# Second norm of a transformer block: the last expert's rows stay on chip and reach their tokens through TensorE, the other experts' sums are added in PSUM

## The chip, the core and the metric

One core of a Trainium2 chip runs the whole block. Measured is the device time of one execution in microseconds (us); the kernel before has a median of 1298.9 us over three runs (1298.69 to 1301.45). Engines are called PE or TensorE (matrix products), ACT or ScalarE, DVE or VectorE, POOL or GpSimd and SP (which only issues DMAs). Each runs its own list of instructions strictly in order and waits on semaphores for the others.

## The reference

One layer: a mixer of sparse attention and gated linear attention, a layer norm, a mixture of 32 experts (two for each token), a second layer norm. What the change touches is the end:

```python
h = layer_norm(DEEPNORM_ALPHA * h + mix, ln1_g[l], ln1_b[l])
...
y = lax.ragged_dot(jax.nn.silu(hg) * hu, w_e_out, sizes)
out = jnp.zeros_like(xt).at[tok_s].add(y * gate_s[:, None].astype(y.dtype))
...
h = layer_norm(DEEPNORM_ALPHA * h + ffn, ln2_g[l], ln2_b[l])
```

There are 1024 tokens of 1024 float32 values. An expert multiplies the rows of its tokens with a 1024x1024 and a 512x1024 matrix; its results, weighted with a gate, are added to the tokens' rows, and the norm is taken over each row.

## The kernel before

The 1024 tokens are 8 tiles of 128. `out_phase` makes the first norm and the router and writes two tables to device memory: `d_h` (the rows, which experts gather) and `d_y` (the rows times alpha, onto which the experts' results are added).

`expert_stream` runs the 32 experts one behind the other, in an order written by hand for PE, ACT and DVE. Each weight piece (1 MB, float32) is loaded by SP, split into a high part on ACT (line 180) and a low part on DVE (line 181), and used in three PE products (line 1351) per 512 columns. `second(e, ...)` makes the second product of expert e, while the first product of expert e+1 is already done; `results` (lines 1398 to 1405) takes the two halves of the 128 result rows out of PSUM, with the gate, one half on ACT (line 1402) and one on DVE (line 1403), into a tile `y`, and POOL issues an indirect DMA that adds them to `d_y` (line 1404). These scatters go one after the other: POOL waits until the one before has landed, since both may add to the same row.

Behind the last expert stands `more_blocks`, a loop (line 1499) that runs only if an expert has more than 128 tokens; here it runs zero times. All engines meet at its entry, and what is behind it starts when the scatter of expert 31 has landed.

`last_norm` then reads `d_y` in 8 loads of 512 KB (line 1558, all issued by SP). While they come, PE spreads the gain and the shift of the norm over 128 partitions, with 8 plain float32 products of 8 partitions and 256 columns (line 1330, issued in `experts`), and ACT copies them from PSUM (line 1565) for POOL. For each tile t the string `LAST[t]` says who does what. Its first letter is the statistics: A on ACT (line 1572 sums the row, line 1575 sums the squares), D on DVE (lines 1581 to 1584). The power -0.5 of the variance is always on POOL (`rstd`, lines 498 and 499). The other two letters are the halves of 512 columns: D stands for two DVE instructions (lines 1602 and 1603), P, G and S for one ACT instruction (line 1605) and two further ones for gain and shift on POOL (line 1610) or DVE (line 1608). The result goes out from the tile by SP (lines 1612 and 1614). The statistics of tile t+1 are begun (`next(gens[t + 1])`) before those of tile t are finished. The order in `last_norm` is that of the program text, but a list scheduler may move instructions within an engine.

## Time and profile before

| | us |
|---|---|
| median of 3 runs | 1298.9 |
| the profiled execution | 1299.05 |
| its span (first to last instruction) | 1297.3 |
| TensorE busy in the span | 1207.5 |
| last product of the last expert issued | 1255.51 |
| scatter of the last expert landed | 1265.72 |
| first load of the last norm issued | 1266.67 |
| end of the span | 1297.3 |

The page gives, for one execution, the busy time of each engine, the span in 40 slices, the chain of waits that ended last, and groups of instructions by source line. Times in the trace count from the start of the span. "PEclk" is the TensorE clock that was granted as a share of 2.4 GHz: 1.00 is 2.4 GHz, 0.50 is 1.2 GHz. A row of the timeline has start, duration, engine, line, operation, output and inputs, shape, and how many instructions were merged into it; matrix products overlap, so that the distance of two starts is what one costs in a stream, not its duration.

### The profile page before, as it was taken

How to read it: one execution, taken by the hardware profiler on the slowest of the kernel's cores; microseconds unless marked ns; L12 is line 12 of the kernel's file. 1: busy time of each engine (PE TensorE's matmuls, PEld its weight loads, DVE VectorE, ACT ScalarE, POOL GpSimd, SP SyncE). 2: the span in 40 equal slices, each digit the busy share in tenths (PEclk: the TensorE clock that was granted, in tenths of full speed). 3: DMA queues.
4: the chain of work that ended last, by engine and by line, in shares of the span. 5: the costliest groups of instructions: out<-in, count | busy, mean ns of one | idle time of the engine just before them, and what ended most of it. 6: DMA issues, size and time to landing. Idle time of an engine off the chain costs nothing.

```text
span 1297.3 us, 19390 instructions
## 1 busy us (share of the span) xinstructions
PE 1207.5 (93%) x6926; PEld 1006.5 (78%) x6926; DVE 1029.1 (79%) x1657; ACT 792.0 (61%) x1111; POOL 388.1 (30%) x350
## 2 busy tenths in 40 slices
PE   6999999999996999999959999999999999999962
PEld 5979989877795888888847888888888888888851
DVE  4567898999993566467768998899988999889855
ACT  4378366665425666122247777777777777777745
POOL 2532642355751453011121312122212222122115
PEclk9999999999997999899969999999999999999985
DMA  7653544324468651784377999999999999999926
GB/s 256 162 180 98 195 156 132 98 70 135 130 172 233 194 163 59 264 295 163 138 274 277 369 365 367 386 368 365 375 358 374 354 357 352 353 357 345 330 68 259
DMA packets 134356, 322.61 MB, mean 249 GB/s; under 512 B 20953, under 2 KB 51570, under 8 KB 134258
## 3 DMA queue, kind: packets, MB, share of 16 engines
q1 hardware_dynamic: 109826, 280.92, 60.8%
q0 software_dynamic: 14848, 25.22, 7.8%
q10 hardware_dynamic: 9584, 15.21, 3.5%
q8 instruction: 55, 0.90, 0.3%
q14 instruction: 43, 0.35, 0.1%
HBM read 283.78 MB, written 54.26 MB: 261 GB/s over the span
## 4 chain that ended last, share of the span: by engine, by line
PE 75%; DVE 9%; DMA 8%; ACT 4%; issue 2%; POOL 1%; SPq 0%; POOLq 0%; ACTq 0%; DVEq 0%
PE acc L1351 25%; PE ot L1351 12%; PE acc L1055 7%; PE acc L236 7%; PE acc L222 6%; DVE eq L722 3%; PE pt L1418 3%; PE s L835 3%; DMA d_y<-y,tok 2%; PE ot L873 2%; PE pt L859 2%; DMA big<-we 2%; PE g L236 1%; PE ot L1070 1%; DMA d_mix<-ym 1%
## 5 line engine op out<-in xcount | busy, mean ns | idle before, releaser
L181 DVE TENSOR_TENSOR elo<-big,ehi 128x2048 fp32r<-128x2048 f32 (+1 forms) x132 | 268.1, 2061 | 22.6 <-ACT ehi L180 21.9
L180 ACT CAST ehi<-big 128x2048 fp32r<-128x2048 f32 (+1 forms) x132 | 223.1, 1727 | 1.9 <-DMA big<-wf 1.2
L1351 PE MATMUL acc<-ehi,xh 128*128 128x512 f32 x512 | 207.4, 405 | 2.0 <-ACT sg L1467 2.0
L1351 PE MATMUL acc<-elo,xh 128*128 128x512 f32 x512 | 204.2, 399 | 0.0
L1351 PE MATMUL acc<-ehi,xl 128*128 128x512 f32 x512 | 204.0, 398 | 0.0
L1425 POOL DMA_INDIRECT xg<-d_h,tok x32 | 36.8, 1150 | 362.4 <-PE pt L1418 361.9
L222 PE MATMUL acc<-big,whi 128*128 128x512 f32 (+1 forms) x384 | 119.4, 390 | 10.5 <-ACT big L180 10.5
L236 PE MATMUL acc<-whi,big 128*128 128x256 f32 x672 | 125.9, 286 | 0.0
L1404 POOL DMA_INDIRECT d_y<-y,tok x32 | 93.0, 2906 | 109.7 <-ACT ehi L180 50.3
L1351 PEld LDWEIGHTS acc<-ehi,xh 128*128 128x128 f32 x512 | 97.3, 190 | 24.7 <-ACT sg L1467 2.4
L1351 PEld LDWEIGHTS acc<-ehi,xl 128*128 128x128 f32 x512 | 97.2, 190 | 23.8 <-DVE xl L181 0.3
L1351 PEld LDWEIGHTS acc<-elo,xh 128*128 128x128 f32 x512 | 97.6, 191 | 22.1
L236 PEld LDWEIGHTS acc<-whi,big 128*128 128x128 f32 x672 | 106.1, 192 | 1.9 <-issue 1.2
L722 DVE TENSOR_SCALAR_CACHE_REDUCE eq<-sc,cand 128x384 bf16<-128x384 f32 (+1 forms) x124 | 100.5, 811 | 6.9 <-POOL sc L734 4.6
L1351 PE MATMUL ot<-ehi,ah 128*128 128x512 f32 x256 | 104.1, 407 | 0.4 <-ACT ah L180 0.4
L181 DVE TENSOR_TENSOR elo<-slot,ehi 128x2048 fp32r<-128x2048 f32 (+1 forms) x46 | 95.6, 2101 | 9.2 <-ACT ehi L180 9.0
L1351 PE MATMUL ot<-ehi,al 128*128 128x512 f32 x256 | 101.6, 397 | 0.4 <-DVE al L181 0.4
L1351 PE MATMUL ot<-elo,ah 128*128 128x512 f32 x256 | 101.5, 396 | 0.0
L236 PE MATMUL acc<-wlo,big 128*128 128x256 f32 x336 | 95.9, 286 | 0.0
L752 ACT ACTIVATE sn<-sc,cand 128x896 bf16<-128x896 f32 (+1 forms) x62 | 67.9, 1095 | 45.8 <-DVE cand L748 34.9
L222 PEld LDWEIGHTS acc<-big,whi 128*128 128x128 f32 x384 | 71.7, 191 | 25.4 <-ACT big L180 10.5
L1055 PE MATMUL acc<-wohi,m 128*128 128x512 f32 x256 | 87.8, 413 | 0.0
(295 smaller groups left out, 2598.0 us busy)
## 6 DMA issues: line engine op xcount, KB each, us to landing
big<-we SPq DMA_DIRECT2D x79, 1024.0 KB, 17.5
big<-wf SPq DMA_DIRECT2D x40, 1024.0 KB, 21.3
slot<-we SPq DMA_DIRECT2D x26, 1024.0 KB, 19.5
sc<-we SPq DMA_DIRECT2D x20, 1024.0 KB, 15.8
slot<-wf SPq DMA_DIRECT2D x16, 1024.0 KB, 14.0
wraw<-wi SPq DMA_DIRECT2D x52, 256.0 KB, 3.2
sc<-wf SPq DMA_DIRECT2D x8, 1024.0 KB, 12.9
raw<-xT SPq DMA_DIRECT2D x8, 512.0 KB, 6.9
```

Of the source, the lines that this page charges most:

```text
L180: nc.scalar.copy(hi, src)
L181: (lo_eng or nc.vector).tensor_tensor(lo, src, hi.bitcast(F32), op=OP.subtract)
L222: nc.tensor.matmul(ps[:m, :n], l[:, j, c0:c0 + m], r[:, j % 2, t0:t0 + n], start=(j == 0 and a == 0), stop=(j == 7 and a == 2))
L236: nc.tensor.matmul(ps[:, i, :], l[:, j % 2, s], r[:, j, :], start=(j == 0 and a == 0), stop=(j == 7 and a == 2))
L722: nc.vector.tensor_scalar(gtt[:, :WS[i]], x, v, 0.0, op0=op, op1=OP.add, accum_out=cnt[:, i:i + 1])
L752: nc.scalar.activation(jnk[:, :WS[i]], y[i], AF.Sign, bias=c, accum_out=cnt[:, i:i + 1])
L835: nc.tensor.matmul(ps[:, 512 * c:512 * c + mm], lq, kk[hd][:, a, c0:c0 + mm], start=a == 0, stop=a == 1)
L1055: nc.tensor.matmul(ps, l[:, j, :], w[:, j, s], start=(j == 0 and a == 0), stop=(j == 7 and a == 2))
L1351: nc.tensor.matmul(o, x[:, jj, :], w[:, j, s], start=(jj == 0 and a == 0), stop=(jj == n - 1 and a == 2))
L1404: nc.gpsimd.indirect_dma_start(out=self.d_y, out_offset=bass.IndirectOffsetOnAxis(ap=tok.bitcast(U32), axis=0), in_=y, in_offset=None, bou ...
L1418: self.last_mm = nc.tensor.transpose(pt[:, 128 * i:128 * i + 128], src[:, 128 * (b + i):128 * (b + i) + 128], self.c["ident"])
L1425: self.last_gather = nc.gpsimd.indirect_dma_start(out=xg, out_offset=None, in_=self.d_h, in_offset=bass.IndirectOffsetOnAxis(ap=tok.bitcas ...
```

## The change

Expert 31 no longer scatters. `places` (called in the middle of its second product) makes, on DVE, for each of the 8 token tiles a 128x128 matrix `sel` of zeros and ones that says which of the expert's rows belongs to which token, and has SP load gain and shift, broadcast to 128 partitions, into a weight buffer that is free by then. `keep_rows` takes the expert's result rows out of PSUM as a high part (ACT) and a low part (DVE) into an SBUF tile `y31`. Expert 30 takes both halves of its rows out on ACT.

`last_norm` has its own PSUM: one pair of banks `sh` for the shift (4 products instead of 8; the gain is now read from SBUF) and three pairs `r2` for tiles of 128x1024. `last_expert()` puts `sel` times `y31` into the next pair (four products of 512 columns, in the one-pass float32r format of the experts' products); `others(t)` adds the tile of `d_y` to it (two plain float32 products of 512 columns with the identity matrix). The statistics and the first step of the normalisation read the sum from PSUM. `last_expert` is called for the first three tiles ahead of everything, and for tile t+3 after the work on tile t. The loads of `d_y` are issued by SP and ACT in turn. In `LAST` the last tile is "ASS" instead of "AGS". The slots of `raw_of` in the loop that runs zero times are shifted by two. The diff, without `raw_of` and the moved banks:

```diff
-LAST = ("ADP", "DDD", "APP", "DDD", "ADD", "ADD", "ADD", "AGS")
+LAST = ("ADP", "DDD", "APP", "DDD", "ADD", "ADD", "ADD", "ASS")
...
-            self.results(ys, cols(e))
+            if e < NE - 1:
+                self.results(ys, cols(e), e == NE - 2)
+            else:
+                self.keep_rows(ys, cols(e)[1])
...
-        second(NE - 1, last)
-
-    def results(self, ys, cols):
+        second(NE - 1, last, self.places)
+
+    def places(self):
+        nc = self.nc
+        self.y31 = self.big(F32R)
+        self.sel = self.big(F32R)[:, 0].rearrange("p (t c) -> p t c", c=128)
+        for t in range(NT):
+            nc.vector.tensor_scalar(self.sel[:, t, :], self.c["iota"], self.lists[:, NE - 1, 0:1], float(PAD - 128 * t),
+                                    op0=OP.subtract, op1=OP.is_equal)
+        self.gain, self.shift = self.slots[8][:, 0], self.slots[8][:, 1]
+        for i, o in enumerate((self.gain, self.shift)):
+            nc.sync.dma_start(o, self.I["l2"][i:i + 1].to_broadcast([128, D]))
+
+    def keep_rows(self, ys, gate):
+        nc = self.nc
+        for h in range(2):
+            s = slice(512 * h, 512 * h + 512)
+            hi, lo = self.y31[:, 0, s], self.y31[:, 1, s]
+            nc.scalar.activation(hi, ys[h], AF.Copy, scale=gate)
+            nc.vector.scalar_tensor_tensor(lo, ys[h], gate, hi.bitcast(F32), op0=OP.mult, op1=OP.subtract)
+
+    def results(self, ys, cols, act=False):
...
-        nc.vector.tensor_scalar(y[:, 512:], ys[1], gate, None, op0=OP.mult)
+        if act:
+            nc.scalar.activation(y[:, 512:], ys[1], AF.Copy, scale=gate)
+        else:
+            nc.vector.tensor_scalar(y[:, 512:], ys[1], gate, None, op0=OP.mult)
...
-                nc.sync.dma_start(r, self.d_y[t * 128:(t + 1) * 128])
+                (nc.sync, nc.scalar)[t % 2].dma_start(r, self.d_y[t * 128:(t + 1) * 128])
...
-            both = p.tile([128, 2, D], F32, name="both")
-            for i, ps in enumerate((gain, shift)):
+            shift = self.bank("sh", [128, D])
+            for c in range(4):
+                nc.tensor.matmul(shift[:, 256 * c:256 * c + 256], ident[0:8, 4 + c:5 + c].to_broadcast([8, 128]), self.l2,
+                                 start=True, stop=True)
+
+            def last_expert():
+                t = len(xs)
+                x = self.bank("r2", [128, D])
                 for k in range(2):
-                    nc.scalar.copy(both[:, i, 512 * k:512 * k + 512], ps[k])
+                    s = slice(512 * k, 512 * k + 512)
+                    for a in range(2):
+                        nc.tensor.matmul(x[:, s], self.sel[:, t, :], self.y31[:, a, s], start=a == 0, stop=False)
+                xs.append(x)
+
+            def others(t):
+                for k in range(2):
+                    s = slice(512 * k, 512 * k + 512)
+                    nc.tensor.matmul(xs[t][:, s], ident, rs[t][:, s], start=False, stop=True)
...
-                    nc.scalar.activation(jnk, rs[t], AF.Copy, scale=-1.0 / D, accum_out=f[:, 0:1])
+                    nc.scalar.activation(jnk, x, AF.Copy, scale=-1.0 / D, accum_out=f[:, 0:1])
...
+            for _ in range(3):
+                last_expert()
...
-                        nc.vector.scalar_tensor_tensor(r[:, s], r[:, s], f[:, 0:1], gain[k], op0=OP.add, op1=OP.mult)
-                        nc.vector.scalar_tensor_tensor(r[:, s], r[:, s], f[:, 2:3], shift[k], op0=OP.mult, op1=OP.add)
+                        nc.vector.scalar_tensor_tensor(r[:, s], x[:, s], f[:, 0:1], gain[:, s], op0=OP.add, op1=OP.mult)
+                        nc.vector.scalar_tensor_tensor(r[:, s], r[:, s], f[:, 2:3], shift[:, s], op0=OP.mult, op1=OP.add)
                     else:
-                        nc.scalar.activation(r[:, s], r[:, s], AF.Identity, scale=f[:, 2:3], bias=f[:, 3:4])
...
+                        nc.scalar.activation(r[:, s], x[:, s], AF.Identity, scale=f[:, 2:3], bias=f[:, 3:4])
+                        nc.gpsimd.tensor_tensor(r[:, s], r[:, s], gain[:, s], op=OP.mult)
+                        if kinds[k] == "S":
+                            nc.vector.tensor_tensor(r[:, s], r[:, s], shift[:, s], op=OP.add)
+                        else:
+                            nc.gpsimd.tensor_tensor(r[:, s], r[:, s], self.shift[:, s], op=OP.add)
...
+                if len(xs) < NT:
+                    last_expert()
```

Up to the second product of expert 31 the engines' lists are the same. From the end of the loop on, PE's list before holds only the products for gain and shift (`l2row` is gain and shift as 8 rows of 256, `K` the constants with the identity):

```order
L1330 MATMUL acc<-l2row,K 128x256 x2
L1330 MATMUL ot<-l2row,K 128x256 x2
L1330 MATMUL acc<-l2row,K 128x256 x2
L1330 MATMUL ot<-l2row,K 128x256 x2
```

Of the change it begins as follows (`big` are `sel` and `y31`, `r` a loaded tile, `r_12264`, `r_12269`, `r_12274` and `r_12298` the PSUM sums of tiles 0 to 3; in square brackets what is waited for, the DMAHW ones being the loads):

```order
L1586 MATMUL sh<-l2row,K 128x256 x4
L1596 MATMUL r_12264<-big 128x512 x4
L1596 MATMUL r_12269<-big 128x512 x4
L1596 MATMUL r_12274<-big 128x512 x4
L1603 MATMUL r_12264<-r,K 128x512 [waits DMAHW1_49]
L1603 MATMUL r_12264<-r,K 128x512
L1603 MATMUL r_12269<-r,K 128x512 [waits DMAHW2_49]
L1603 MATMUL r_12269<-r,K 128x512
L1603 MATMUL r_12274<-r,K 128x512 [waits DMAHW3_49]
L1603 MATMUL r_12274<-r,K 128x512
L1596 MATMUL r_12298<-big 128x512 [waits Activation_49]
L1596 MATMUL r_12298<-big 128x512 x3
```

New are all rows from the second on; tile 3 takes the banks of tile 0, and waits for ACT's last read of them. The products with `y31` for tiles 3 to 7 wait in turn for ACT (tile 0's banks), DVE (1), ACT (2), DVE (3), and DVE and ACT (4).

POOL's list in the last norm, from the power of tile 1 to that of tile 4, before (`f` holds the statistics of a tile, two rows to a power; `both` is the copied gain and shift):

```order
L498 TENSOR_SCALAR f<-f 128x1
L499 TENSOR_TENSOR f<-f,mhalf 128x1
L1610 TENSOR_TENSOR r<-r,both 128x512 x2
L498 TENSOR_SCALAR f<-f 128x1
L499 TENSOR_TENSOR f<-f,mhalf 128x1
L1598 TENSOR_TENSOR f<-f 128x1
L498 TENSOR_SCALAR f<-f 128x1
L499 TENSOR_TENSOR f<-f,mhalf 128x1
L498 TENSOR_SCALAR f<-f 128x1
L499 TENSOR_TENSOR f<-f,mhalf 128x1
L1610 TENSOR_TENSOR r<-r,both 128x512 x4
```

The same stretch of the change (`sc` is the buffer with gain and shift):

```order
L1648 TENSOR_TENSOR r<-r,sc 128x512
L500 TENSOR_SCALAR f<-f 128x1
L1652 TENSOR_TENSOR r<-r,sc 128x512
L501 TENSOR_TENSOR f<-f,mhalf 128x1
L1640 TENSOR_TENSOR f<-f 128x1
L1648 TENSOR_TENSOR r<-r,sc 128x512 x2
L1652 TENSOR_TENSOR r<-r,sc 128x512
L500 TENSOR_SCALAR f<-f 128x1
L1652 TENSOR_TENSOR r<-r,sc 128x512
L501 TENSOR_TENSOR f<-f,mhalf 128x1
```

The powers of tiles 3 and 4 stood ahead of the four 128x512 steps of tile 2; now that of tile 3 (the last two rows with `f`) ends behind all four, and that of tile 4 after it.

DVE's list of the change at that place (`r_12298` and `r_12320` are the sums of tiles 3 and 4, `sh` the shift):

```order
L1644 SCALAR_TENSOR_TENSOR r<-r_12298,f,sc 128x512 [waits DMAHW4_49,DVE_49]
L1644 SCALAR_TENSOR_TENSOR r<-r_12298,f,sc 128x512
L1645 SCALAR_TENSOR_TENSOR r<-r,f,sh 128x512 [waits DVE_49,Pool_49]
L1645 SCALAR_TENSOR_TENSOR r<-r,f,sh 128x512 [waits DVE_49]
L1644 SCALAR_TENSOR_TENSOR r<-r_12320,f,sc 128x512 [waits DMAHW5_49,PE_49,Activation_49]
L1644 SCALAR_TENSOR_TENSOR r<-r_12320,f,sc 128x512
```

The rows of tile 4, which read its banks, stand behind those of tile 3 that wait for POOL; before, the same pair read an SBUF tile that nobody waited to reuse.

## Rows read from the trace of the kernel before

**Rows 1.** The chain of waits that ended last, in order of time, around the end of the experts: start, duration, engine or DMA, output and line.

```profile
1234.55 31.17 DMA d_y<-y,tok
1265.72 0.02 issue
...
1267.54 6.20 DMA r<-d_y
```

**Rows 2.** Timeline of POOL's last two scatters, of the ACT and DVE instructions that take the last two experts' rows out of PSUM, and of ACT's first split of expert 31's second weights.

```profile
1251.82 1.54 POOL L1404 DMA_INDIRECT d_y<-y,tok  x1 [15.45 <-DVE y L1403]
1258.91 1.54 POOL L1404 DMA_INDIRECT d_y<-y,tok  x1 [5.54 <-issue]
...
1249.22 0.69 ACT L1402 ACTIVATE y<-ot,lists 128x512 f32<-128x512 f32 x1
1255.23 0.69 ACT L1402 ACTIVATE y<-ot,lists 128x512 f32<-128x512 f32 x1 [5.33 <-PE ot L1351]
...
1250.35 0.74 DVE L1403 TENSOR_SCALAR y<-ot,lists 128x512 f32<-128x512 f32 x1
1255.94 0.75 DVE L1403 TENSOR_SCALAR y<-ot,lists 128x512 f32<-128x512 f32 x1 [4.85 <-PE ot L1351]
...
1244.00 2.00 ACT L180 CAST ehi<-big 128x1024 fp32r<-128x1024 f32 x2 [1.20 <-DMA big<-wf]
```

**Rows 3.** A window of 1 us behind the last product: busy time (and count) of PE, PE's weight loads, DVE, ACT and POOL, then the granted TensorE clock, the busy share of the DMA engines and GB/s.

```profile
1258.00:1259.00 1.00, 0.00 (x0) 0.00 (x0) 0.00 (x0) 0.00 (x0) 0.09 (x1) 0.54 0.00 0
```

**Rows 4.** Timeline from the loads of the last norm to its first statistics.

```profile
1266.67 4.01 SPq L1558 DMA_DIRECT2D r<-d_y  x8
1267.35 2.07 PE L1330 MATMUL acc<-l2row,K 8*128 8x256 f32 x4 [11.45 <-issue]
1270.26 1.06 ACT L1572 ACTIVATE jnk<-r 128x1024 f32<-128x1024 f32 x1 [0.22 <-DMA r<-d_y]
1272.63 1.91 PE L1330 MATMUL ot<-l2row,K 8*128 8x256 f32 x4
```

**Rows 5.** A window of 2 us in the last norm; the columns are those of rows 3.

```profile
1272.00:1274.00 2.00, 2.00 (x6) 1.44 (x5) 1.70 (x5) 1.73 (x4) 0.76 (x2) 0.50 1.00 408
```

**Rows 6.** Timeline of PE at the full clock: eight records of four plain float32 products of 128 columns (line 557) and the product behind them; two products of an expert.

```profile
82.28 1.06 PE L557 MATMUL g<-Kin,loga 128*128 128x128 f32 x8
83.09 0.72 PE L482 MATMUL acc<-K,Q 128*128 128x512 f32 x2
...
1252.93 0.39 PE L1351 MATMUL ot<-ehi,ah 128*128 128x512 f32 x1
1253.16 0.39 PE L1351 MATMUL ot<-elo,ah 128*128 128x512 f32 x1
```

**Rows 7.** Timeline of PE when the experts begin, at the half clock: two products that follow each other.

```profile
668.95 0.63 PE L1351 MATMUL acc<-ehi,xh 128*128 128x512 f32 x1
669.37 0.63 PE L1351 MATMUL acc<-elo,xh 128*128 128x512 f32 x1
```

**Rows 8.** Windows of 1 us around three restarts of TensorE; the columns are those of rows 3.

```profile
404.00:405.00 1.00, 0.15 (x2) 0.15 (x2) 0.00 (x0) 0.99 (x5) 0.00 (x0) 0.50 0.62 217
408.00:409.00 1.00, 1.00 (x7) 0.68 (x7) 0.71 (x3) 0.64 (x3) 0.00 (x0) 0.92 1.03 387
...
528.00:529.00 1.00, 1.00 (x6) 1.00 (x6) 0.01 (x1) 0.11 (x1) 0.00 (x0) 0.50 1.09 246
534.00:535.00 1.00, 1.00 (x5) 0.82 (x4) 0.00 (x0) 0.00 (x0) 0.00 (x0) 0.77 1.05 434
...
682.00:683.00 1.00, 0.60 (x3) 0.16 (x1) 1.00 (x2) 0.98 (x2) 0.00 (x0) 1.00 0.09 37
...
684.00:685.00 1.00, 0.41 (x1) 0.41 (x2) 1.00 (x2) 1.00 (x2) 0.00 (x0) 0.82 0.59 225
688.00:689.00 1.00, 1.00 (x5) 0.79 (x5) 0.00 (x0) 0.00 (x0) 0.00 (x0) 0.97 1.03 422
```

**Rows 9.** Groups of instructions in the last norm: busy time, mean ns of one, and the idle time before them.

```profile
L1610 POOL TENSOR_TENSOR r<-r,both 128x512 f32<-128x512 f32 x8 | 10.0, 1267 | 2.3 <-ACT r L1605 2.2
L1575 ACT ACTIVATE jnk<-r,f 128x1024 f32<-128x1024 f32 x6 | 6.8, 1138 | 0.0
L1572 ACT ACTIVATE jnk<-r 128x1024 f32<-128x1024 f32 x6 | 6.3, 1046 | 0.5 <-DMA r<-d_y 0.5
L1602 DVE SCALAR_TENSOR_TENSOR r<-r,f,acc 128x512 f32<-128x512 f32 x6 | 4.5, 743 | 0.5 <-ACT jnk L1575 0.5
L499 POOL TENSOR_TENSOR f<-f,mhalf 128x1 f32<-128x1 f32 x8 | 4.4, 551 | 0.6
L1605 ACT ACTIVATE r<-r,f 128x512 f32<-128x512 f32 x5 | 3.8, 800 | 1.9 <-POOL f L1598 1.9
L498 POOL TENSOR_SCALAR f<-f 128x1 f32<-128x1 f32 x8 | 1.5, 191 | 13.3 <-ACT jnk L1575 12.7
L1565 ACT COPY both<-acc 128x512 f32<-128x512 f32 x2 | 1.2, 577 | 13.5 <-PE acc L1330 13.5
```

**Rows 10.** Timeline of the last instructions.

```profile
1290.78 2.48 POOL L1610 TENSOR_TENSOR r<-r,both 128x512 f32<-128x512 f32 x2 [1.63 <-ACT r L1605]
1292.07 0.69 DVE L1608 TENSOR_TENSOR r<-r,ot 128x512 f32<-128x512 f32 x1 [1.21 <-POOL r L1610]
1292.79 0.83 SPq L1612 DMA_DIRECT2D out<-r  x2
```

More of the change, by code (lines that the diff above doesn't have):

```diff
@@ L356, in run @@
                     self.attention(ap, before)
-            self.banks(ctx, "ps3", acc=3, ot=3, pt=2)
-            self.out_phase(ctx, outw)
-            outc.close()
-            self.experts()
+            with ExitStack() as ps:
+                self.banks(ps, "ps3", acc=3, ot=3, pt=2)
+                self.out_phase(ctx, outw)
+                outc.close()
+                self.experts()
+            self.last_norm()
             if "mix" in (self.upto if isinstance(self.upto, tuple) else ()):
@@ L1322, in experts @@
             work.close()
-            l2 = []
-            for i in range(2):
-                ps = [self.bank(b, [128, 512]) for b in ("acc", "ot")]
-                for k in range(2):
-                    for j in range(2):
-                        c = 4 * i + 2 * k + j
-                        nc.tensor.matmul(ps[k][:, 256 * j:256 * j + 256], self.c["ident"][0:8, c:c + 1].to_broadcast([8, 128]),
-                                         self.l2, start=True, stop=True)
-                l2.append(ps)
-        self.last_norm(*l2)
     def expert_stream(self, cols, x, work):
@@ L1536, in raw_of @@
             def raw_of(q, src, c0, last):
-                raw = self.slots[(c0 + 2 * q) // 2]
+                raw = self.slots[2 + (c0 + 2 * q) // 2]
                 for j in range(2):
@@ L1549, in more_blocks, with last_norm @@
             nc.vector.tensor_scalar(turn, turn, 1.0, None, op0=OP.add)
-    def last_norm(self, gain, shift):
+    def last_norm(self):
         nc = self.nc
-        with self.pool("last") as p:
-            rs, fs = [], []
+        gain, ident = self.gain, self.c["ident"]
+        with ExitStack() as banks, self.pool("last") as p:
+            self.banks(banks, "ps4", sh=1, r2=3)
+            rs, fs, xs = [], [], []
             for t in range(NT):
                 r = p.tile([128, D], F32, name="r", bufs=NT)
-                nc.sync.dma_start(r, self.d_y[t * 128:(t + 1) * 128])
+                (nc.sync, nc.scalar)[t % 2].dma_start(r, self.d_y[t * 128:(t + 1) * 128])
@@ L1567, in stats @@
             def stats(t):
                 f = p.tile([128, 4], F32, name="f", bufs=NT)
+                others(t)
+                x = xs[t]
                 if LAST[t][0] == "A":
                     jnk = p.tile([128, D], F32, name="jnk", bufs=2)
-                    nc.scalar.activation(jnk, rs[t], AF.Copy, scale=-1.0 / D, accum_out=f[:, 0:1])
+                    nc.scalar.activation(jnk, x, AF.Copy, scale=-1.0 / D, accum_out=f[:, 0:1])
                     yield
                     jnk = p.tile([128, D], F32, name="jnk", bufs=2)
-                    nc.scalar.activation(jnk, rs[t], AF.Square, bias=f[:, 0:1], accum_out=f[:, 1:2])
+                    nc.scalar.activation(jnk, x, AF.Square, bias=f[:, 0:1], accum_out=f[:, 1:2])
@@ L1580, in stats @@
                     for k in range(2):
-                        nc.vector.bn_stats(st[:, k, :], rs[t][:, 512 * k:512 * k + 512])
+                        nc.vector.bn_stats(st[:, k, :], x[:, 512 * k:512 * k + 512])
                     nc.vector.bn_aggr(f[:, 0:2], st)
@@ L1589, in last_norm @@
             for t in range(NT):
-                r = rs[t]
+                r, x = rs[t], xs[t]
                 if t + 1 < NT:
@@ L1601, in last_norm @@
                     if kinds[k] == "D":
-                        nc.vector.scalar_tensor_tensor(r[:, s], r[:, s], f[:, 0:1], gain[k], op0=OP.add, op1=OP.mult)
-                        nc.vector.scalar_tensor_tensor(r[:, s], r[:, s], f[:, 2:3], shift[k], op0=OP.mult, op1=OP.add)
-                    else:
-                        nc.scalar.activation(r[:, s], r[:, s], AF.Identity, scale=f[:, 2:3], bias=f[:, 3:4])
-                        for i, (ps, op) in enumerate(((gain, OP.mult), (shift, OP.add))):
-                            if kinds[k] == "GS"[i]:
-                                nc.vector.tensor_tensor(r[:, s], r[:, s], ps[k], op=op)
-                            else:
-                                nc.gpsimd.tensor_tensor(r[:, s], r[:, s], both[:, i, s], op=op)
+                        nc.vector.scalar_tensor_tensor(r[:, s], x[:, s], f[:, 0:1], gain[:, s], op0=OP.add, op1=OP.mult)
+                        nc.vector.scalar_tensor_tensor(r[:, s], r[:, s], f[:, 2:3], shift[:, s], op0=OP.mult, op1=OP.add)
+                    else:
+                        nc.scalar.activation(r[:, s], x[:, s], AF.Identity, scale=f[:, 2:3], bias=f[:, 3:4])
[4 more added lines that the diff above has]
+                            nc.gpsimd.tensor_tensor(r[:, s], r[:, s], self.shift[:, s], op=OP.add)
                     if t == NT - 1:
```

## The prediction

> **What bounds the kernel now.** I read the chain of waits first. Up to TensorE's last product (1255.51) the change moves almost nothing. Behind it the chain is one DMA, the adding scatter of the experts' rows, until 1265.72 [rows 1]. The timeline shows why: expert 30's scatter is issued at 1251.82, and POOL can issue that of expert 31 only at 1258.91, when the first has landed [rows 2]; that one lands 6.81 later. Then 0.95 to the first load of the last norm (1266.67) and 1.63 to TensorE's first product (1267.35) [rows 4]. From the first statistics (1270.26) to the end of the span (1297.3) it is 27.0 us, in which ACT, DVE and POOL share the work and TensorE has nothing but 7.2 us of spreading gain and shift. So the reader is to see two stages: about 10 us of waiting for a scatter, which the change attacks, and a norm of 27 us, into which the change puts TensorE.
>
> **The wait that goes.** Expert 30's scatter becomes the last. Its rows are taken out by ACT at 1249.22 and by DVE at 1250.35, behind DVE's low part of the activations; on ACT alone the second half follows the first and ends at 1250.5 instead of 1251.09, so the issue moves from 1251.82 to 1251.2. Its transfer ended by 1258.2 (no traffic in the window from 1258 [rows 3]), 6.4 after its issue; so it lands at 1257.6. The other condition of the loop's entry is DVE's second low part: high parts on ACT at 1255.2 and 1255.9 (0.69 each), low parts on DVE behind each, priced as the 0.75 of 1255.94 [rows 2], end 1257.4. TensorE starts at 1257.6 + 1.6 = 1259.2, the loads at 1258.6: **8.1 us earlier**. Whoever reads 6.8 for the landing adds 0.4.
>
> Hidden around it: the eight `sel` steps on DVE lie in its 4.85 us of waiting [rows 2]; no row shows them; between nothing and the 0.75 of a step of 512 columns they take 0 to 6 us, at the worst end 0.4 too long. The loads of gain and shift queue behind the last weights; the last second-product weights came 1.20 late for ACT [rows 2], but TensorE needs them only 5 us later. I take 0, and up to 2.6 (1.05 MB at the 408 GB/s of [rows 5]) if they compete. ACT's four load issues lie in its idle time.
>
> **What TensorE gets.** Each plain float32 product leaves two records. At the full clock eight records of four products of 128 columns take 82.28 to 83.09, 0.20 a product [rows 6], so one of 512 columns 0.81, and the two of `others` 1.62 a tile. At the half clock the 16 records of line 1330 (256 columns) start 1267.35 to 1274.1, 0.45 each [rows 4]; 512 columns are 1.8, a tile 3.6. A float32r product of 512 costs 0.23 [rows 6] or 0.42 [rows 7], so `last_expert` 0.94 or 1.7 a tile. Per tile that is **2.56 us at the full and 5.3 at the half clock**: 20 or 42 us for eight tiles, where ACT (six tiles of 1.05 + 1.14, five halves of 0.8) and DVE have some 17 to 19 each [rows 9]. TensorE becomes as heavy as they are, and it stands in front of them.
>
> The clock: it fell at 1258.5, 2.6 us after the last product [rows 3]. In the change TensorE rests at least 3.3 us, so I take it at 0.50 at 1259.2. Then it rises 3.2 to 5.9 us after a dense restart: 404.9 to 408.1, 528.7 to 534.6, 684.6 to 689.0 [rows 8]. The products on 8 partitions I do not count as such a restart: 7.2 us of them ran at 0.50 to the end [rows 5]. (The Trainium skill, page "TensorE: Matmul & The Clock Gate", section "Part 1: The HAM clock gate", says that the clock is throttled by default and that activity releases it, without an exception for few partitions; the row here disagrees, and this would be rival 2.)
>
> **The sum, step by step.** S is the shift, E the products of `y31`, O those of the identity; reads start about 0.2 after the last record.
> S: 8 records of 0.45, 1262.8. Three E: ten products at 0.43, the clock rises at 1267.1 (4.3 after 1262.8), two at 0.23: 1267.6. O of tiles 0, 1, 2: readable at 1269.4, 1271.0, 1272.7. The loads (before: first after 3.6 us, all in some 12) are there by then. So the first statistics start only 0.9 us earlier than before: **7.2 of the 8.1 us are spent**.
> Tile 0: ACT's sum 1270.5, squares 1271.65, POOL's three small steps (0.19, 0.55, 0.19 [rows 9] and gaps of 0.07) 1272.8. But ACT's next instruction is the sum of tile 2, which waits for TensorE until 1272.7 and ends at 1273.75; only then comes the first half of tile 0, 1274.5, and tile 0's banks are free. TensorE has waited 2 us. Tiles 3, 4, 5, 6, at 2.56: 1277.3, 1279.8, 1282.4, 1284.9.
> Tile 7 needs the banks of tile 4, and here the new wait sits. POOL's power of tile 3 is queued behind four steps of tile 2 (1.25 each, 1267 ns in [rows 9]). These start when ACT has done tile 2's first half at 1278.9 (POOL is kept by a step of tile 0 until 1277.2, then power 1278.1, then ACT 0.8). Power of tile 3: 1278.9 + 5.0 + 0.7 = 1284.6. DVE waits for it with the shift of tile 3 (to 1286.0), and behind that in its list stand the two reads of tile 4's banks (0.66 each in a stream, 743 ns in [rows 9]): free at 1287.3. TensorE, done at 1284.7, waits 2.6; tile 7 is readable at 1290.1.
> End: ACT's sum of tile 7 1291.2, squares of tile 6 (queued ahead) 1292.35, of tile 7 1293.5; POOL 1294.65; ACT's two halves 1295.4 and 1296.1; POOL's two gains 1296.7 and 1297.95; DVE's last shift 1298.6. Before, the last arithmetic ended at 1293.26 and the span 4.05 later [rows 10]. **Span 1302.7**, 5.4 longer than 1297.3.
> The two dropped copies of the gain (0.58 each [rows 9]) shorten ACT, which now waits for TensorE; worth 0. Reading PSUM in place of SBUF I take at the same price: a copy of 512 from PSUM took 0.58, the scaled one from SBUF 0.80 [rows 9]; ten such reads on the chain give -1 to +1.
> The execution was 1299.05 with a span of 1297.3, so 1.75 lies outside; its time stands 0.15 above the median. 1302.7 + 1.75 - 0.15 = **1304.3**.
> Its own range: rise after 3.2 or 5.9 in place of 4.3, -0.5 to +0.8; landing +0.4; reads -1 to +1; loads of gain +2.6; and if the clock falls in the 2.6 us wait before tile 7 (as after the stops at 682.6 and 1255.9 [rows 3, 8]), tile 7 at 5.3 in place of 2.56, +2.7. Together 1302 to 1309.
>
> **Rivals.** What can be told from no change is 0.2%, 2.6 us: 1296.3 to 1301.5 is "the same".
> 1. The clock is still up when TensorE restarts (the rest is 3.3 us, not the 11.5 of [rows 4]). S costs 1.8, E 2.8, tile 0 is readable at 1265.6, everything moves up by 3.8: 1300.5, the same. Against: the falls of [rows 3, 8] came 2.6 and 2.2 us after a stop.
> 2. The eight-partition products do count, and the clock rises at 1259.2 + 4.3 = 1263.5: 1.7 less, 1302.6. Against: the row of 7.2 us [rows 5]. (That is the page's rule.)
> 3. The clock never rises, because float32 passes with zeros and ones don't raise it or the bank waits pull it down: S 3.6, E 5.1, O 10.8 to 1278.7; tile 0's banks at 1280.3; five tiles of 5.3 to 1306.8, and the 12.8 of the end: 1319.6, 1321 in time. For: TensorE has run no long float32 stream at 128 partitions before. Against: the E products alone are 5 us of what raised it three times.
> 4. Faster: the clock is up and no bank ever holds TensorE, since ACT, DVE and POOL clear tile t before t+3 is wanted. From 1263.8 eight O and five E take 17.7, 1281.5; with 0.2 and 12.6 of end the span is 1294.3, 1295.9 in time. It decides from the point where the three bank waits together are below about 0.5 us. Against: the lists of ACT and POOL, in which the power of tile 3 stands behind tile 2. That the scatter leaves the chain is sure from POOL's list, so "it doesn't do what it says" has no chance worth one.
>
> **How the numbers follow.** Forecast 0.53 (all slower), rival 1 0.18, rival 2 0.10, rival 3 0.08, rival 4 0.11. Slower by over 0.2%: 0.53 + 0.10 + 0.08 less 0.03 for the low edges, 0.68; same 0.18 + 0.03, 0.21; faster 0.11. The range leaves out rivals 3 and 4 (0.19) and reaches from rival 1 less the 1.0 of the PSUM reads, 1299.5, to the forecast's upper end with 2 us for clock falls at the other waits: 1311.
>
> **What will show it.** First load near 1258.6 and TensorE near 1259.2; clock 0.50 there and 1.00 from about 1267; records of line 1603 some 0.4 apart at 512 columns; first statistics near 1269.4; TensorE idle before tiles 3 and 7; POOL's power of tile 3 behind tile 2's steps. Wrong would be: a clock of 1.00 at 1259, float32 products under 0.8, or no wait for banks.

## The result and the profile after

The changed kernel takes 1308.09 us (median of 9 runs, 1304.83 to 1309.78) beside 1300.48 for the kernel before on the same chip (9 runs, 1298.49 to 1304.90): a ratio of 1.0063, 95% interval 1.0049 to 1.0076. It is slower, by about 8 us. I had forecast a ratio of 1304.3 / 1298.9 = 1.0042, about 5.4 us.

The profiled execution of the changed kernel has a span of 1303.0 us, close to the forecast 1302.7; part of that is luck. Its experts ended 2.62 us earlier than those of the profile of before (start of the last product 1252.89, before 1255.51), and such shifts of some us are seen from one execution to the next. So I compare only the **stretch from the start of the last expert's last product to the end of the span**: 1297.3 - 1255.51 = 41.8 before, 1303.0 - 1252.89 = 50.1 after. The difference of 8.3 is 0.64% of 1298.9, which is what the ratio says. In every run below the stretch and the ratio agree to about 0.2%. That is up to 2 us, so a difference of this size between two kernels rests on one execution of each.

The timeline of PE in the changed kernel, from the last product on (line 1586 is the shift, 1596 the products of `y31`, 1603 the identity products), and ACT's first statistics:

```profile
1252.89 0.39 PE L1342 MATMUL ot<-ehi,al 128*128 128x512 f32 x1
1256.76 3.78 PE L1586 MATMUL sh<-l2row,K 8*128 8x256 f32 x8 [3.48 <-issue]
1260.47 5.49 PE L1596 MATMUL r<-big 128*128 128x512 f32 x12
1265.76 5.62 PE L1603 MATMUL r<-r,K 128*128 128x512 f32 x12
1273.25 1.19 PE L1596 MATMUL r<-big 128*128 128x512 f32 x4 [1.87 <-ACT r L1647]
1274.28 1.88 PE L1603 MATMUL r<-r,K 128*128 128x512 f32 x4
1275.60 1.49 PE L1596 MATMUL r<-big 128*128 128x512 f32 x4
1276.92 1.88 PE L1603 MATMUL r<-r,K 128*128 128x512 f32 x4
...
1286.65 1.86 PE L1596 MATMUL r<-big 128*128 128x512 f32 x4 [2.56 <-DVE r L1644]
1288.31 2.85 PE L1603 MATMUL r<-r,K 128*128 128x512 f32 x4
...
1267.98 1.02 ACT L1612 ACTIVATE jnk<-r 128x1024 f32<-128x1024 f32 x1 [13.97 <-DMA r<-d_y]
```

It answers to [rows 4]: there TensorE restarted at 1267.35, 11.84 after the last product, and the first statistics stood 2.91 behind that. Now it restarts 3.87 after the last product, and the first statistics (ACT, 1267.98) come 11.22 behind that. TensorE waits twice for banks, 1.87 before tile 3 and 2.56 before tile 7. Between the waits a tile costs 2.64 (1274.28 to 1276.92), products and adds together.

Windows of 1 us of the changed kernel, with the columns of [rows 3]; the clock is the seventh value:

```profile
1256.00:1257.00 1.00, 0.24 (x1) 0.24 (x2) 0.00 (x0) 0.00 (x0) 0.00 (x0) 0.57 0.00 0
1257.00:1258.00 1.00, 1.00 (x3) 0.81 (x4) 0.00 (x0) 0.00 (x0) 0.00 (x0) 0.50 1.06 180
...
1265.00:1266.00 1.00, 1.00 (x4) 0.81 (x3) 0.00 (x0) 0.00 (x0) 0.00 (x0) 0.50 1.01 410
1266.00:1267.00 1.00, 1.00 (x3) 0.36 (x3) 0.00 (x0) 0.00 (x0) 0.00 (x0) 0.81 1.06 430
...
1286.00:1287.00 1.00, 0.35 (x1) 0.31 (x2) 1.00 (x2) 0.40 (x2) 0.43 (x2) 0.93 0.96 397
1287.00:1288.00 1.00, 1.00 (x4) 0.78 (x3) 1.00 (x3) 0.00 (x0) 0.31 (x1) 0.50 0.31 127
```

The clock is at its lower level (0.50, 1.2 GHz) from the restart until 1266.4, through the whole shift and all of the first 12 products of `y31`, and once more from 1286.9, behind the wait before tile 7.

The chain of waits of the changed kernel, where it leaves TensorE and comes back to it:

```profile
1277.01 0.79 ACT r L1647
...
1280.38 1.22 POOL r L1652
...
1281.95 1.28 POOL r L1652
1283.24 0.52 POOL f L501
...
1284.44 0.74 DVE r L1645
1285.18 1.33 DVE r L1644 x2
...
1286.65 1.86 PE r L1596 x4
1288.51 2.67 PE r L1603 x4
```

Read it from the bottom: tile 7 (PE) waits for DVE's two reads of tile 4's banks (line 1644); these stand behind the shift of tile 3 (1645), which waits for POOL's power of tile 3 (501), which stands behind POOL's steps of tile 2 (1652), released by ACT's halves of tile 2 (1647). This is the queue that the prediction names.

So the restart came 8.0 us earlier (11.84 to 3.87), and what follows it is 16.3 longer: 46.24 in place of 29.95. Of the 16.3, 8.3 lie ahead of the first statistics and 8.0 behind them.

### The profile page after: what moved, and what is told of

Read it like the earlier page. It is cut to its first block, busy times and chain, and to the rows that moved or that the text cites. A ratio compares the mean times of both kernels' runs of the same rounds, so it can differ in the third digit from the quotient of the medians.

```text
span 1303.0 us, 19507 instructions
## 1 busy us (share of the span) xinstructions
PE 1226.7 (94%) x6982; PEld 1015.6 (78%) x6982; DVE 1030.3 (79%) x1665; ACT 791.3 (61%) x1109; POOL 388.4 (30%) x349
## 4 chain that ended last, share of the span: by engine, by line
PE 78%; DVE 9%; DMA 5%; ACT 4%; issue 2%; POOL 1%; ACTq 0%; another core or an unknown queue 0%; POOLq 0%; SPq 0%; DVEq 0%
PE acc L1342 26%; PE ot L1342 13%; PE acc L1057 7%; PE acc L236 6%; PE acc L222 6%; PE pt L1438 3%; DVE eq L724 3%; PE s L837 3%; PE ot L875 3%; PE pt L861 2%; DMA big<-wf 2%; PE g L236 1%; PE ot L1072 1%; DMA d_mix<-ym 1%; PE g L222 1%
## 5 line engine op out<-in xcount | busy, mean ns | idle before, releaser
L754 ACT ACTIVATE sn<-sc,cand 128x896 bf16<-128x896 f32 (+1 forms) x62 | 67.9, 1095 | 47.8 <-DVE cand L750 37.8
```

Source lines behind the costliest of these rows:

```text
L754: nc.scalar.activation(jnk[:, :WS[i]], y[i], AF.Sign, bias=c, accum_out=cnt[:, i:i + 1])
```

## The experiments

Each run was timed in 5 rounds against the kernel before. The stretch is that of its profiled execution; "restart to end" is its part from TensorE's first product behind the experts (the first of the last norm). Dummies are products whose results nobody reads; those right behind the last product do not count as the restart.

| kernel | stretch | restart to end | ratio to before, 95% |
|---|---|---|---|
| before | 41.8 | 29.95 | 1 |
| changed | 50.1 | 46.24 | 1.0063 (1.0049 to 1.0076) |
| e1 before without the last scatter | 36.2 | 30.96 | 0.9954 (0.9934 to 0.9973) |
| e2 changed, tile 3's power first | 47.5 | 42.96 | 1.0035 (1.0020 to 1.0050) |
| e3 changed, 8 dummies | 46.1 | 41.64 | 1.0050 (1.0033 to 1.0068) |
| e4 changed, no shift products | 47.8 | 44.01 | 1.0032 (1.0018 to 1.0047) |
| e5 changed, last tile on DVE | 48.3 | 43.93 | 1.0051 (1.0035 to 1.0066) |
| e6 changed, cheap add | 44.8 | 41.44 | 1.0026 (1.0016 to 1.0035) |
| e7 dummies, `y31` first, power first | 43.8 | 39.32 | 1.0012 (0.9998 to 1.0027) |
| e8 re-ordered | 41.9 | 37.49 | 0.9989 (0.9975 to 1.0003) |
| e9 re-ordered, clock held | 39.8 | 35.40 | 0.9988 (0.9976 to 1.0001) |
| e10 re-ordered, four pairs of banks | 42.1 | 37.69 | 1.0004 (0.9987 to 1.0022) |

**e1: what the wait alone is worth.** The kernel before, with

```diff
-            self.results(ys, cols(e))
+            self.results(ys, cols(e), e < NE - 1)
...
+        if scatter:
+            nc.gpsimd.indirect_dma_start(out=self.d_y, ...
```

> The kernel before without the scatter of expert 31; it leaves that expert's rows out of the result, the rest is as before. Stretch measured: from the start of the last product of expert 31 to the end of the span, 41.8 us before and 50.1 in the changed kernel. My account (the scatter alone is worth 8 us, and all of it reaches the end if nothing is put in its place): 34.3 to 34.8, ratio 0.994 to before. Rival (most of the scatter's time lies beside something else, the loop's entry or the loads, so that its removal brings little): 39 to 41.8, ratio 0.998 to 1.000.

The stretch is 36.2: the gain is 5.6, between the two theories. Timeline of e1:

```profile
1248.92 1.54 POOL L1405 DMA_INDIRECT d_y<-y,tok  x1 [16.12 <-DVE y L1403]
...
1257.84 2.07 PE L1330 MATMUL acc<-l2row,K 8*128 8x256 f32 x4 [4.84 <-issue]
...
1261.65 0.58 ACT L1566 COPY both<-ot 128x512 f32<-128x512 f32 x1 [1.12 <-PE ot L1330]
1262.13 1.06 ACT L1573 ACTIVATE jnk<-r 128x1024 f32<-128x1024 f32 x1
```

The restart comes 8.92 after the issue of expert 30's scatter (8.57 to 8.90 in the changed kernel and its variants without dummies), so with the last scatter gone the one before it holds the restart. (In the five variants with dummies the restart stands 2.15 behind the dummies, and 4.42 to 4.43 behind the last product, each time: there the dummies seem to hold it, which was not tested.) Then ACT's copies of gain and shift wait for TensorE's half-clock products on 8 partitions. Two of them stand ahead of its first sum where the kernel before has one, so ACT's list in e1 has another order, and the first statistics stand 4.98 behind the first load's issue (1257.15) where before had 3.59 [rows 4]. The wait was real: its removal alone gave 5.6, and in the change it brought the restart 8.0 forward.

**e2: the power of tile 3 ahead of tile 2.**

```diff
                 for _ in gens[t]:
                     pass
+                if t + 1 < NT and LAST[t + 1][0] == "D":
+                    for _ in gens[t + 1]:
+                        pass
...
-                        nc.gpsimd.tensor_tensor(r[:, s], r[:, s], gain[:, s], op=OP.mult)
+                        with self.tc.issue_after(self.last_pow.ins):
+                            nc.gpsimd.tensor_tensor(r[:, s], r[:, s], gain[:, s], op=OP.mult)
```

> The changed kernel, with the statistics of tile 3 finished before the normalisation of tile 2 in the text, and POOL's gain steps ordered behind the power. My account (tile 7 waits 2.6 us for DVE, which waits for the power behind four POOL steps, and the clock falls in that wait): no wait of TensorE before tile 7, clock 1.00 there, tile 7 readable 4.4 us earlier, stretch 45.7 against 50.1, ratio 0.9965 to the changed kernel. Rival (the wait before tile 7 is set by ACT's squares of tile 4, or the time is given back behind it): wait and stretch shorter by under 1.5.

Timeline of e2, POOL and PE:

```profile
1281.09 0.55 POOL L501 TENSOR_TENSOR f<-f,mhalf 128x1 f32<-128x1 f32 x1
1281.61 2.53 POOL L1652 TENSOR_TENSOR r<-r,sc 128x512 f32<-128x512 f32 x2
...
1288.34 1.16 PE L1596 MATMUL r<-big 128*128 128x512 f32 x4 [1.25 <-ACT jnk L1612]
1289.34 1.88 PE L1603 MATMUL r<-r,K 128*128 128x512 f32 x4
```

The power of tile 3 ends 21.5 after the restart, 27.0 in the changed kernel: 5.5 earlier. The wait before tile 7 falls from 2.56 to 1.25 and the clock stays up, so tile 7 takes 2.9 in place of 4.5. From restart to end 3.3 are gained, of the stretch 2.6, where I expected 4.4 and the rival under 1.5. The rest is not there because ACT is late next: its list holds the sum of tile 5 ahead of the squares of tile 4, and DVE's reads of tile 4 wait for these.

**e3: the clock held over the gap.** Eight products of no use, right behind the last one:

```diff
                 self.expert_stream(cols, x, work)
+                pt = self.bank("pt", [128, 512])
+                l, w = self.last_pair
+                for i in range(8):
+                    nc.tensor.matmul(pt, l[:, 3, :], w[:, 1, 512:], start=True, stop=True)
...
+            self.last_pair = l[0], hi
```

> The changed kernel with eight more products of expert 31's second weights, into a PSUM bank that nobody reads, behind its last product, so that TensorE rests under 2 us before the last norm. My account (the half clock at the restart costs 4.7 us): clock 1.00 at the restart, shift 1.85, three tiles of the last expert 2.8, first statistics 4.7 earlier, stretch 45.4 to 47; if the clock still falls during the products on 8 partitions, 48 to 50. Rival (the start of the statistics is set by the loads or by ACT, not by TensorE): stretch 49 to 50 though the clock is 1.00.

Windows of e3 and, below, its timeline of PE:

```profile
1261.00:1262.00 1.00, 1.00 (x6) 0.74 (x4) 0.00 (x0) 0.00 (x0) 0.00 (x0) 1.00 0.73 262
1262.00:1263.00 1.00, 1.00 (x4) 0.72 (x3) 0.00 (x0) 0.00 (x0) 0.00 (x0) 0.59 0.99 385
1263.00:1264.00 1.00, 1.00 (x3) 0.76 (x3) 0.00 (x0) 0.00 (x0) 0.00 (x0) 0.50 0.93 365
```

```profile
1256.07 2.04 PE L1325 MATMUL pt<-ehi,ah 128*128 128x512 f32 x8
1260.26 1.99 PE L1591 MATMUL sh<-l2row,K 8*128 8x256 f32 x8 [2.15 <-issue]
1262.18 4.58 PE L1601 MATMUL r<-big 128*128 128x512 f32 x12
```

At the restart the clock is up and the shift costs 1.99 in place of 3.78. But it falls at 1262.2, when TensorE has been busy for 2 us with products on 8 partitions, and the products of `y31` begin at the lower level. The first statistics stand 8.3 behind the restart (11.22 in the changed kernel), the stretch is 4.0 shorter. That is inside the range I expected, but not for the reason alone that I gave: 2.4 of it stand ahead of the first statistics, and 1.6 come from tile 7 (2.97 from its first product to its first sum, 4.61 in the changed kernel), because the clock stayed up in the wait before it, which the dummies do not touch. The ratio gives back less, 1.0050; the 1.0033 of the stretch is the lower end of its interval.

**e4: no shift products.** DVE reads the shift from SBUF:

```diff
-            self.banks(banks, "ps4", sh=1, r2=3)
+            self.banks(banks, "ps4", r2=3)
...
-            shift = self.bank("sh", [128, D])
...
+            shift = self.shift
```

> The changed kernel without the four products that spread the shift: DVE reads it from the buffer that is loaded anyway. My account (TensorE is first in the chain, so its 3.7 us count whole): first statistics 3.7 earlier, stretch 46.4. If the clock also rises the earlier since no eight-partition products stand ahead, the same; if these products did count as activity, the clock rises the later and the gain is 2 to 3 us. Rival (DVE reads slower from SBUF beside POOL, or the chain starts at the loads): gain under 1 us.

The clock now rises at 1265.0, 5.9 after the restart (1259.09, with `y31`); in the changed kernel it rose at 1266.4, 5.9 after the first product of `y31` too, but 9.6 after the restart with the shift. The first statistics are 3.7 earlier, as forecast, yet the stretch is only 2.3 shorter: the 3.7 are still there when tile 3's products begin, 3.0 when those of tile 7 do, and 2.3 when the arithmetic ends. What is lost is lost where DVE and POOL hinder each other. (A gain of 2 to 3 was also expected if the products on 8 partitions count for the clock; against that stands where it rose.) Timeline of e4, DVE and POOL in one place:

```profile
1272.57 1.85 DVE L1642 SCALAR_TENSOR_TENSOR r<-r,f,sc 128x512 f32<-128x512 f32 x2
...
1273.30 0.51 POOL L500 TENSOR_SCALAR f<-f 128x1 f32<-128x1 f32 x1
1273.90 1.68 POOL L1649 TENSOR_TENSOR r<-r,sc 128x512 f32<-128x512 f32 x1
```

Two steps of DVE that read two operands from SBUF took 1.85, where 1.40 is usual with one operand in PSUM, and POOL's steps 0.51 and 1.68 in place of 0.19 and 1.27.

**e5: the last tile on DVE.** `LAST[7]` is "DDD" in place of "ASS".

> The changed kernel with the last tile wholly on DVE (statistics from batch-norm steps, both halves by the two DVE steps) in place of ACT's sum, squares and halves, POOL's gain and DVE's shift. The theory that the tail is the chain of engines behind the last product (in the changed kernel the last arithmetic ended 8.5 us after the tile could be read: sum 1.2, squares twice 1.3, power, halves 1.45, POOL's gain 1.25 each, shift 0.69) expects 5.1 after it: batch-norm steps 1.5, power about 0.8, four DVE steps of 0.7. So the stretch from the start of the last expert's last product to the end of the span falls from 50.1 to 46 to 47 us, and the ratio to the kernel before by 0.002 to 0.003. The rival: DVE is behind with tiles 4 to 6 by then (each costs it 2.8 us), the last tile waits for them, and the stretch stays at 49 or more.

The stretch is 48.3, between the two. Timeline of DVE in e5:

```profile
1290.43 2.72 DVE L1644 SCALAR_TENSOR_TENSOR r<-r,f,sc 128x512 f32<-128x512 f32 x4
1293.07 2.71 DVE L1645 SCALAR_TENSOR_TENSOR r<-r,f,sh 128x512 f32<-128x512 f32 x4
1295.70 1.29 DVE L1621 BATCH_NORM_STATS2 bnst<-r 128x6 f32<-128x512 f32 x2
```

Tile 7 could be read at 1293.86; DVE was still at tiles 5 and 6 until 1295.70. The last arithmetic ended 6.3 after the tile could be read (8.6 in the changed kernel), of which 1.8 is this wait: the tail was a chain of engines, and DVE's lateness took part of the gain.

**e6: the add at the price of a float32r product** (the output lacks the other experts' rows).

```diff
-                    nc.tensor.matmul(xs[t][:, s], ident, rs[t][:, s], start=False, stop=True)
+                    nc.tensor.matmul(xs[t][:, s], self.sel[:, t, :], self.y31[:, 1, s], start=False, stop=True)
```

> The changed kernel in which the plain float32 identity product that adds the other experts' rows is replaced by a third float32r product of the same width (the low part once more), so the other experts' rows are left out of the output; the loads and all else stay. A float32r product of 512 columns takes 0.23 us at the full clock and 0.42 at half, the float32 one 0.8 and 1.8 or less, so each tile's two adds cost 0.5 or 0.85 instead of 1.3 or 2.9. If TensorE's adds lie on the path at both ends (first statistics, last tile), the stretch from the start of the last product falls from 50.1 to 47 to 48: about 1 at the first statistics and 1 to 2 at the last tile. The rival, that the middle is set by DVE and POOL and only the last tile's add counts: 48.5 to 49.5. With the float32 work gone TensorE may also be less busy, so that the clock falls in more places; the windows tell.

The stretch is 44.8: 5.3 shorter, twice what I expected. Timeline of PE in e6:

```profile
1268.16 1.63 PE L1603 MATMUL r<-big 128*128 128x512 f32 x6
...
1287.68 1.05 PE L1603 MATMUL r<-big 128*128 128x512 f32 x2
```

The first three adds took 5.62 and take 1.63; I had counted only tile 0's. The third is tile 2's, whose halves on ACT release POOL's queue: they stand 3.5 earlier (16.7 behind the restart, 20.25), POOL's power of tile 3 3.2, and the last tile's add gives 1.8 more.

**e7: the products of `y31` first.** e2 and e3 together, and the shift moved behind the adds of tiles 0 and 1:

```diff
+            def spread():
...
                     next(gens[t + 1])
+                if t == 0:
+                    with self.tc.issue_after(self.add_mm.ins):
+                        spread()
```

> The changed kernel with the two edits tried one by one before (tile 3's power ahead of tile 2's gain steps; 8 dummy products behind the last one), and the 8-partition shift products moved behind the adds of tiles 0 and 1, so that the 128-partition products of expert 31 come first at the restart. The theory: the clock is still up at the restart and 8-partition products do not hold it up, while the 128-partition ones do, so the 12 products take 2.8 us instead of 5.5, the first add 1.3, and the first statistics stand 4 to 5 us after the restart (11.2 in the changed kernel, 8.3 with the dummies alone); from restart to end 35 to 39 us instead of 46.2, the stretch from the last product 40 to 44. The rival: the first statistics are bound by the rows' loads or the clock falls all the same in the first products; then first statistics at 7 or more after the restart and a stretch of 44.5 or more.

43.8, and 39.3 from restart to end: at the upper edge of what was expected. The first statistics stand 7.1 behind the restart, since the first add now waits for the load (timeline of PE in e7, and a window of 1 us):

```profile
1256.58 4.51 PE L1604 MATMUL r<-big 128*128 128x512 f32 x12 [2.15 <-issue]
1261.69 3.70 PE L1611 MATMUL r<-r,K 128*128 128x512 f32 x8 [0.60 <-DMA r<-d_y]
...
1256.00:1257.00 1.00, 0.42 (x1) 0.43 (x2) 0.00 (x0) 0.00 (x0) 0.00 (x0) 0.68 0.60 57
```

Both sides had a share: the clock was down all the same from 1256.4 to 1259.8, 3.2 behind the restart (0.68 in the window 1256 to 1257), and the rows' load is the next bound, 5.9 after its issue.

**e8: and the other engines' lists.** e7, the last tile on DVE, tile 5's second half on ACT and POOL (`LAST[5]` "ADP"), the early power for tile 3 alone, and on ACT a tile's squares ahead of the next sum:

```diff
-                if t + 1 < NT:
-                    next(gens[t + 1])
                 for _ in gens[t]:
                     pass
+                if t + 1 < NT:
+                    next(gens[t + 1])
```

> The one before, and besides: the last tile on DVE, tile 5's second half on ACT and POOL instead of DVE, and on ACT each tile's squares ahead of the next tile's sum. Bound by TensorE from tile to tile (2.65 us each) with short waits for banks, tile 7 can be read about 27 us after the last product, and DVE ends it 5 to 6 later, the end 3 after that: a stretch of 36 to 39.5 us against 41.8 in the kernel before and 50.1 in the changed one, so 2 to 5 us faster than the kernel before, ratio 0.996 to 0.9985. If the road through TensorE costs more than the scatter it saves (5.6 us) however it is ordered, the stretch is 42 or more and the ratio 1.000 or above.

41.9, no better than before, and the ratio (0.9989, 0.9975 to 1.0003) does not tell it from before either; the expectation was missed by 2.4. Timeline of PE in e8, and a window of 1 us:

```profile
1257.11 3.03 PE L1604 MATMUL r<-big 128*128 128x512 f32 x12 [2.15 <-issue]
1262.08 5.40 PE L1611 MATMUL r<-r,K 128*128 128x512 f32 x8 [1.94 <-DMA r<-d_y]
...
1262.00:1263.00 1.00, 0.92 (x2) 0.49 (x3) 0.00 (x0) 0.00 (x0) 0.00 (x0) 0.90 1.00 348
```

TensorE now waits 1.94 for the load, the clock falls just behind that wait (0.90 in the window 1262 to 1263, then 0.50 until 1266.2), and the adds of tiles 0 and 1 take 5.40. Behind that TensorE has no gap at all: it is the bound.

**e9: the clock held over the load.** e8, with eight dummies into the bank of the shift:

```diff
             gens = [stats(t) for t in range(NT)]
+            for i in range(8):
+                nc.tensor.matmul(shift[:, :512], self.sel[:, 2, :], self.y31[:, 0, :512], start=True, stop=True)
```

> The re-ordered kernel (e8) with 8 dummy 128-partition float32r products more, between expert 31's products and the first add, into the bank that the shift overwrites later. In e8 TensorE waited 1.94 us there for the first tile's load, and the granted clock was 0.50 from that wait on for about 3.5 us, so that the adds of tiles 0 and 1 took 5.40 instead of the 2.7 that four full-clock tiles show. The theory that the clock was lost in that wait and is held by 128-partition products expects those adds at 3.0 or less, the first statistics 1 to 1.5 earlier, TensorE's chain, which was without a gap from there on, 2 to 2.7 earlier, and a stretch from the last product to the end of 39 to 40.5 instead of 41.9. The rival: the adds are paced by the loads that still stream then, not by the clock; the stretch stays at 41.5 or more.

```profile
1262.65 1.98 PE L1639 MATMUL sh<-big 128*128 128x512 f32 x8
1264.46 3.59 PE L1611 MATMUL r<-r,K 128*128 128x512 f32 x8
1267.99 1.99 PE L1594 MATMUL sh<-l2row,K 8*128 8x256 f32 x8
```

The timeline of PE in e9 shows the same adds in 3.59 (I expected 3.0 or less; at 0.88 a product the four take 3.5), the clock is 1.00 through all of TensorE's work, and the stretch is 39.8 as expected, 2.0 below the kernel before. The ratio, 0.9988 (0.9976 to 1.0001), lies between 3.1 us faster and 0.1 slower; it tells e9 neither from e8 nor from the kernel before.

**e10: four pairs of banks, no shift products.**

> The re-ordered kernel (e8) without the shift products (DVE reads the shift from SBUF), with the two banks given to a fourth pair for the tiles, so that four tiles' products of expert 31 stand ahead of the first add, with 4 dummies among them. TensorE then has 1.9 us less to do on its gapless chain and, the clock being held, 2.7 less in the first adds: tile 7 readable 27 to 28 us after the last product instead of 31.9. If TensorE bounds, the stretch is 37 to 39. The rival: DVE and POOL become the bound, since DVE's second step took 0.92 instead of 0.70 and POOL's power 0.94 to 1.05 instead of 0.55 when DVE read SBUF alone; then DVE has no gap from tile 4 on, and the stretch is 40 or more, no better than e9.

Tile 7 can be read 28.1 behind the last product, as forecast for TensorE, but the stretch is 42.1: DVE worked without a gap from 1270.74 to 1284.9 and ended at 1296.6. Timeline of DVE and POOL in e10:

```profile
1280.10 2.83 DVE L1652 SCALAR_TENSOR_TENSOR r<-r,f,sc 128x512 f32<-128x512 f32 x2
...
1279.43 2.96 POOL L1656 TENSOR_TENSOR r<-r,sc 128x512 f32<-128x512 f32 x2
1282.35 1.74 POOL L1660 TENSOR_TENSOR r<-r,sc 128x512 f32<-128x512 f32 x1
```

Two of DVE's steps that took 1.40 with one operand in PSUM take 2.83, and POOL's 1.27 becomes 1.74. Its rival won.

## Why the prediction was right, and where it was off

The direction and the mechanism were right: the scatter leaves the chain, TensorE takes its place in front of the statistics, at the half clock, and the banks make it wait twice. The size fell short by 2.9 of 8.3: ahead of the first statistics I had 7.2 of the 8.1 us spent, and all of the 8.0 were, and 0.3 more. The forecast's steps, counted from the start of the last product (1255.51 in the forecast, 1252.89 measured):

| step | forecast | measured |
|---|---|---|
| TensorE restarts | 3.7 | 3.9 |
| shift done | 7.3 | 7.6 |
| three tiles' `y31` done | 12.1 | 13.1 |
| first statistics | 13.9 | 15.1 |
| tile 3's products begin | 19.0 | 20.4 |
| POOL's power of tile 3 ends | 29.1 | 30.9 |
| tile 7's products begin | 31.8 | 33.8 |
| tile 7 readable | 34.6 | 38.4 |
| last arithmetic ends | 43.1 | 47.0 |
| end of the span | 47.2 | 50.1 |

- **The wait that goes**: 8.1 forecast, 8.0 measured, in part by luck. POOL issued expert 30's scatter 0.3 behind its rows (1248.08, rows out at 1247.81) where I took 0.7, and by the chain of waits it landed 7.1 after its issue (1255.17) where I took 6.4; the two errors cancel. e1 adds that expert 30's scatter is the next bound of it. The eight `sel` steps, which no row showed, took 1.70 on DVE (1247.73) and cost nothing.
- **The clock at the restart**: 0.50 as forecast. It rose 5.9 behind the first product of `y31`, where I took 4.3: so all of these products and the start of tile 0's add ran at the half clock, 0.9 of the 2.9. Two windows of [rows 3, 8] I had misread: a mean of 0.54 from 1258 to 1259 puts the fall at 1258.1, not 1258.5, and 0.97 from 688 to 689 puts that rise at 688.1, 3.5 behind its restart. Neither figure stands in the sum itself.
- **A tile at the full clock**: 2.64 in place of 2.56, right to 4%; over four tiles 0.3. A plain float32 product of 512 columns takes 0.88 in a stream (four in 3.53 in e9, eight in 7.13 in e10), where I took 0.81 from [rows 6].
- **POOL's queue and the wait before tile 7**: 2.6 forecast, 2.56 measured, and e2 shows the cause: with the power ahead of the queue it is 1.25, and then ACT's squares hold it.
- **The term that was mis-sized most** is tile 7 "readable at 1290.1", that is 2.8 behind the wait; it took 4.6. I had put the fall of the clock in that wait (+2.7) into the range, not into the sum. In e4 and e5 too the clock fell in this wait (2.58), in e3 it stayed up through 2.55, so this 1.8 is there in some executions and not in others; in the profiled one it is most of the 2.9.
- **The end**: the last arithmetic stands 8.6 behind the readable tile (8.5 forecast); the write behind it took 3.2 where before took 4.05, which gave 0.9 back. Reading PSUM in place of SBUF, for which I allowed -1 to +1, cost nothing: ACT's sum takes 1.02 (1.06 before), the squares 1.11 (1.15), a half 0.77 (0.80).
- **Rival 1** (the clock still up) was wrong: 0.50 at 1257. With work in the gap it was up at the restart in e3, e8, e9 and e10, but not in e7. **Rival 2** (8 partitions count) was wrong: the changed kernel's shift ran at 0.50 to its end, the clock rose 5.9 behind the first full-width product both with the shift ahead and without it (e4), and in e3 a clock that was up fell after 2 us of such products. The Trainium skill, page "TensorE: Matmul & The Clock Gate", section "Part 1: The HAM clock gate", says that activity releases the throttle and excepts no products; these rows do not agree with it. What it is about these products (8 partitions, 256 columns) that makes the difference, no run here tells. **Rival 3** (it never rises) was wrong: 1.00 from 1267 on, with float32 products of zeros and ones. **Rival 4** (no bank wait) was wrong: 1.87 and 2.56.

What the runs add to the prediction is where the 16.3 behind the restart lie. 10.8 of them (46.24 to 35.40) go away in e9 without any of the added arithmetic going: by the order of POOL's, ACT's and TensorE's lists, the last tile's engine, and the clock in two gaps. The other 5.4 stay: TensorE's chain of 25.4 without a gap (1259.80 to 1285.18 in e9) and DVE's 6.8 behind it. Against 7.4 by which e9 restarts earlier that leaves 2.0. So in the best order that was tried the idea is worth about 2 us by one profile, and between 3.1 and -0.1 by the ratio; the order that it was given costs 10. The steps between (e2, e3, e4, e5, e6) overlap and don't add up one by one; e7 and e8 were measured as sums, so the share of the single edits in them was not told apart.

## What to carry to other kernels

An engine that comes to stand in front of all the others should be priced at the clock it will have there. Here work that ran at the lower clock, 3.8 us of it on 8 partitions, stood ahead of everything; full-width products first, and products of no use in two gaps, had the clock at 1.00 all through e9, though in e7 one filled gap was not enough. When a buffer is held until another engine has read it, follow that engine's list back over its own waits (here TensorE, DVE, POOL, ACT): the length of a queue two engines away set the wait, and taking it away (e2) showed the next engine's list behind it. Compare profiles by a stretch that begins at a common event, not by the span.

## What was not expected of the hardware

- The products on 8 partitions and 256 columns never saw the clock rise (3.78 us of them at 0.50 in the changed kernel, 7.2 in [rows 4, 5]), and in e3 it was down at 1262.2 after a gap of 2.15 and 2 us of them, where full-width products in their place ran at 1.00 in e8, e9 and e10. Between full-width products 2 us of them did no harm (e9, 1.00).
- The same gap of 2.15 us between dummies and restart left the clock up in e3, e8, e9 and e10, and in e7 it was down from 1256.4, 0.2 ahead of the restart. One execution each was profiled.
- DVE's step on two tensors and POOL's steps slow each other when DVE reads both tensors from SBUF (e4: 1.85 for 1.40, 1.68 for 1.27; e10: 2.83 for 1.40). The Trainium skill, page "SBUF — State Buffer", section "Who interferes with whom", says that a DVE instruction with two SBUF inputs contends with a GpSimd instruction that reads SBUF; these rows agree.
